# A decoder trunk on one core: a feed-forward in two phases with one wide matmul for both activation parts

## The chip, the cores and the metric

One core of one Trainium2 chip runs the whole program in one launch. The metric is device microseconds of one execution.

## What is computed

Four layers, each a feed-forward, a mixer and a second feed-forward, on 256 tokens of 1024 channels in float32. The mixers are in turn a gated recurrence with a short convolution (RG), forgetting attention (fox), a causal convolution module with 31 taps (conv), and RG again. Cut to what matters here:

```python
D_MODEL = 1024; BATCH = 1; SEQ = 256; DEPTH = 4; D_FF = 2816; CV_KERNEL = 31

def _rms_norm(x, g):
    y = x * lax.rsqrt(jnp.mean(x * x, axis=-1, keepdims=True) + EPS)
    return y * g

def _swiglu(x, w_in, w_out):
    gate, up = jnp.split(x @ w_in, 2, axis=-1)
    return (jax.nn.silu(gate) * up) @ w_out

# layer i
x = x + 0.5 * _swiglu(_rms_norm(x), w_in_1, w_out_1)
x = x + Mixer_{i mod 3}(_rms_norm(x))
x = x + 0.5 * _swiglu(_rms_norm(x), w_in_2, w_out_2)
```

## The kernel before, in words

x lies transposed: eight blocks of 128 channels (partitions) by 256 tokens. A weight block is 128x128 and stays in TensorE while tokens stream through it, so one matmul has 256 columns. For float32 accuracy each float32 operand is split into a high part, which the matmul takes whole, and a low part, the rest. A product of a weight block and activations then takes three matmuls: high weights on high activations, high weights on low activations, low weights on high activations.

**Weights.** Two feeds bring them in the order of use: `wi` for input weights, 1 MB chunks [128x2048], and `wo` for output weights, 512 KB chunks [128x1024]. `split_steps` (L92) makes the high part on ScalarE (ACT, L105) and the low part on VectorE (DVE, L108) as raw minus high. Some chunks are split in parts of 1024 or 512 columns. `ahead` (L122) splits up to a given depth and issues the next loads on SyncE's queue.

**A feed-forward stage** (`ffn`, L373) has 22 steps. Step p computes the gate and up block of hidden block p: `in_unit` (L298, matmuls in `in_steps`, L292), 8 input blocks x 2 x 3 = 48 matmuls into one bank of PSUM; then `out_unit` (L332, matmuls at L317) of hidden block p - 3, 8 x 3 = 24 matmuls which add to the four banks `o0` to `o3`. Between them `evac` multiplies by the norm (L379, 128x512), takes Silu on ScalarE (L381), multiplies by up (L383) and splits the result in `yh` (L385, ScalarE) and `yl` (L386, VectorE). `out_tail` (L336) finishes the last two hidden blocks, updates x (L352) and prepares the next stage: high part of x (L198), square (L211), low part (L224), sum of squares (`acc`, L218, folded at L220).

**The norm.** The input matmuls take x without its norm; the scale of each token is applied in `evac`. `norm_stat` (L260) sums the squares over the partitions with a matmul of ones against `acc` (128x256, every partition gets the same sums), computes z (L266) and an inverse root by three rounds of Newton's method (L246, then L255 to L257) on 128x256. Only VectorE's L379 waits for that.

**Mixers.** RG and conv use `in_unit` and `out_unit` as well. RG's four taps are on VectorE (L490). In conv (L974) the 8 x 31 taps are shared: 105 on VectorE (L1007, L1009), 72 as a ScalarE scale (L1021) with a GpSimd add (L1023), 71 on TensorE (L1030) as float32 matmuls against diagonal matrices, which GpSimd builds in `conv_setup` (L967) during the feed-forward before. `centre` (L1094) subtracts the bias of the layer norm and the statistics matmuls follow (L1104). In fox, `v_unit` runs 512-column matmuls (L685): there activations are the stationary operand and weights stream. Its two loops over heads carry the splits of the next stage's chunks as side work (`next_weights`).

The order of the work is written out by hand in all of this: each engine runs its instructions in the order of the program, and `plan` gives the engines of each split.

Of the kernel before, what the change touches and what calls it, by code (L numbers as in the profile page):

```python
# [60 lines left out]
N_IN = DEPTH * 2 * NF + 2 * 8 + 12 + 8  # L61
N_OUT = DEPTH * 2 * NF + DEPTH * KD


class Feed:


    def __init__(self, nc, src, n, width, pool, raw_bufs, part_bufs, tag):
        self.nc, self.src, self.n, self.width = nc, src, n, width
        self.pool, self.raw_bufs, self.part_bufs, self.tag = pool, raw_bufs, part_bufs, tag  # L70
        self.raw, self.parts, self.plan, self.pieces, self.spare = {}, {}, {}, {}, {}
        self.nd = self.ns = self.nu = 0
# [14 lines left out]
    def cuts(self, i):  # L87
        n = self.pieces.get(i, 1)
        w = self.width // n
        return [slice(j * w, (j + 1) * w) for j in range(n)]  # L90

    def split_steps(self):  # L92

        nc, i = self.nc, self.ns
        self.load(i + 1)
        raw = self.raw.pop(i)
        hi, lo = (self.pool.tile([P, self.width], F32R, tag=self.tag + x, bufs=self.part_bufs,
                                 name=f"{self.tag}{x}{i}") for x in "hl")
        self.parts[i] = (hi, lo)
        self.ns += 1  # L100
        cast, rest = self.plan.get(i, ("act", "dve"))
        rest = nc.gpsimd if rest == "pool" else nc.vector
        for c in self.cuts(i):
            if cast == "act":
                nc.scalar.activation(hi[:, c], raw[:, c], AF.Copy)  # L105
            else:
                nc.vector.tensor_copy(hi[:, c], raw[:, c])
            rest.tensor_tensor(lo[:, c], raw[:, c], hi[:, c].bitcast(F32), op=ALU.subtract)  # L108
            yield

    def split(self, upto):
        while self.ns < min(upto, self.n):
            for _ in self.split_steps():
                pass

    def take(self):
        self.split(self.nu + 1)
        r = self.parts.pop(self.nu)
        self.nu += 1
        return r  # L120

    def ahead(self, depth):  # L122
        self.split(self.nu + depth)
        self.load(self.ns + self.raw_bufs)


class Trunk:
# [3 lines left out]
    def build(self, pools):  # L131
# [3 lines left out]
        self.seq = 0  # L135
        self.sq = {}
        self.fin = Feed(nc, self.ap["win"], N_IN, 2 * D, self.wpool, 2, 3, "wi")
        self.fout = Feed(nc, self.ap["wout"], N_OUT, D, self.wpool, 3, 3, "wo")
        self.x = [c.tile([P, 2, T], F32, name=f"x{b}") for b in range(4)]
        self.vec = c.tile([P, NVEC], F32, name="vec")  # L140
        for i, t in zip((2, 3), self.slabs(2)):
            self.fin.spare[i] = t[:, :2 * D]
# [3 lines left out]
        self.fin.pieces[0] = 4  # L146
        self.fin.load(1, lambda j: load_x(j) if j else None)
        self.fin.pieces[1] = 2
        self.fin.load(4)
        nc.sync.dma_start(self.vec[:, KD:], self.ap["vec"][:, KD:])  # L150
        self.fout.load(2)
# [4 lines left out]
        self.fin.plan[0] = FIRST  # L156
        self.fout.plan[0] = self.fout.plan[1] = ("act", "dve")
        first = self.fin.split_steps()
        for b in range(4):
            self.prep_hi(b, 0, False)  # L160
            next(first)
            self.prep_sq(b, 0, True)
            self.prep_lo(b, 0)
        for _ in first:
            pass
        self.fin.split(2)
        for s in range(self.nsub):
            l, part = divmod(s, 3)
            last = s == self.nsub - 1
            for i in (2, 3) if s else (3,):  # L170
                self.fin.plan[self.fin.nu + i] = ("act", "dve")
            if part != 1:
                hook = None
                if s == 0:
                    hook = self.setup_lambda()
                elif s + 1 < self.nsub and part == 0 and MIXERS[l][0] == 2:
                    hook = self.conv_setup()
                self.ffn(s, last, hook, 1 if s == 0 else 6)
            else:
                kind, slot = MIXERS[l]  # L180
                (self.rg, self.fox, self.conv)[kind](s, slot, last)

# [6 lines left out]
    def prep_hi(self, b, s, sq=True):  # L189

        nc = self.nc
        if b == 0:
            self.xh, self.xl = ([self.work.tile([P, 2, T], F32R, tag=f"x{p}{i}", bufs=1,
                                                name=f"x{p}{s}_{i}") for i in range(4)]
                                for p in "hl")
            self.acc = self.work.tile([P, 2, T], F32, tag="acc", bufs=1, name=f"acc{s}")
        for j in range(2):
            nc.scalar.activation(self.xh[b][:, j], self.x[b][:, j], AF.Copy,  # L198
                                 scale=self.v(f"norm{s}", 2 * b + j))
        if sq:  # L200
            self.prep_sq(b, s)

    def prep_sq(self, b, s, pool=False):
        nc = self.nc
        sq = self.acc
        if b:
            sq = self.work.tile([P, 2, T], F32, tag="sq", bufs=2, name=f"sq{s}_{b}")
        if pool:
            nc.gpsimd.tensor_tensor(sq, self.x[b], self.x[b], op=ALU.mult)
        else:  # L210
            nc.scalar.activation(sq, self.x[b], AF.Square)  # L211
        self.sq[b] = sq

    def prep_acc(self, b):

        nc = self.nc
        if b:
            nc.vector.tensor_tensor(self.acc, self.acc, self.sq[b], op=ALU.add)  # L218
        if b == 3:
            nc.vector.tensor_tensor(self.acc[:, 0], self.acc[:, 0], self.acc[:, 1], op=ALU.add)  # L220

    def prep_lo(self, b, s):
        for j in range(2):
            self.nc.vector.scalar_tensor_tensor(self.xl[b][:, j], self.x[b][:, j],  # L224
                                                self.v(f"norm{s}", 2 * b + j),
                                                self.xh[b][:, j].bitcast(F32),
                                                op0=ALU.mult, op1=ALU.subtract)
        self.prep_acc(b)

    def pr(self, shape=None):  # L230
        self.seq += 1
        return self.psum.tile(shape or [P, 2, T], F32, tag="pr", bufs=3, name=f"pr{self.seq}")

    def st(self, shape):
        self.seq += 1
        return self.psum.tile(shape, F32, tag="st", bufs=1, name=f"st{self.seq}")
# [23 lines left out]
    def norm_stat(self):  # L260

        nc = self.nc
        ps = self.st([P, T])
        nc.tensor.matmul(ps, self.ones, self.acc[:, 0], start=True, stop=True)
        z = self.tmp([P, T], "h", 2)
        nc.vector.tensor_scalar(z, ps, 1.0 / D, EPS, op0=ALU.mult, op1=ALU.add)  # L266
        self.r_b = self.rsqrt(z, [P, T], "r")

    def norm_start(self):
        self.fin.ahead(2)  # L270
        self.norm_stat()
# [8 lines left out]
    def xk(self, k):  # L280
        return self.xh[k // 2][:, k % 2], self.xl[k // 2][:, k % 2]

    def in_steps(self, ps, ahead=2):
        nc = self.nc
        hi, lo = self.fin.take()
        hi = hi.rearrange("p (k j c) -> p k j c", k=KD, j=2)
        lo = lo.rearrange("p (k j c) -> p k j c", k=KD, j=2)
        for k in range(KD):
            xh, xl = self.xk(k)
            for j in range(2):  # L290
                for i, (w, m) in enumerate(((hi, xh), (hi, xl), (lo, xh))):
# [3 lines left out]
            yield  # L295
        self.fin.ahead(ahead)

    def in_unit(self, hook=None, at=2, ahead=2):  # L298
        ps = self.pr()
        for k, _ in enumerate(self.in_steps(ps, ahead)):  # L300
            if hook and k + 1 == at:
                hook()
        return ps

    def bank(self, b):
        self.seq += 1
        return self.psum.tile([P, 2, T], F32, tag=f"o{b}", bufs=1, name=f"o{b}_{self.seq}")
# [3 lines left out]

    def out_mm(self, m, w, y, first, last, which=(0, 1, 2)):
        hi, lo = w
        yh, yl = y
        for i, (wt, mv) in enumerate(((hi, yh), (hi, yl), (lo, yh))):
# [5 lines left out]
    def out_steps(self, y, first, ahead=True, late=False):  # L321
        w = self.fout.take()
# [932 lines left out]
```

## Time and profile before

| | |
|---|---|
| runs | 2031.32 us median of 3 (2031.09 to 2031.87) |
| profiled execution | 2032.03 us |
| its span | 2030.3 us |
| mean granted clock of TensorE | 0.984 |
| busy, share of span | TensorE 96%, VectorE 68%, ScalarE 47%, GpSimd 6% |
| DMA | 338 MB, mean 167 GB/s |

The span runs from the first to the last instruction; 1.7 us of the execution lie outside it. A busy time is the sum over the engine's instructions, with overlaps counted once. In the rows, PE is TensorE, DVE VectorE, ACT ScalarE, POOL GpSimd. A granted clock of 1.00 is 2.4 GHz, 0.50 is 1.2 GHz.

### The profile page before, as it was taken

The page shows a single profiled execution, that of the slowest core. Times are in us where ns is not written, and L with a number is a line of the kernel's source. Part 1 is how long each engine was busy: PE and PEld are TensorE (multiplying, and loading weights), DVE is VectorE, ACT ScalarE, POOL GpSimd, SP SyncE. Part 2 cuts the span into 40 slices and gives each one's busy share as a digit, 9 for nine tenths or more (in the row PEclk, how much of TensorE's full clock was granted, in tenths as well). Part 3 has the DMA queues.
Part 4 walks back from the last instruction along what each step waited for, and adds up shares of the span by engine and source line. Part 5 has one row for each costly group of instructions (what it writes and reads, how often), then busy time and mean ns, then how long its engine had stood idle before and what let it go on. Part 6 is the DMA issues. An engine that isn't in the chain of part 4 may idle for free.

```text
span 2030.3 us, 36907 instructions
## 1 busy us (share of the span) xinstructions
PE 1955.5 (96%) x15618; PEld 1912.5 (94%) x15618; DVE 1389.9 (68%) x1909; ACT 952.2 (47%) x1258; POOL 121.2 (6%) x169
## 2 busy tenths in 40 slices
PE   7999979999999999999999998779999999979998
PEld 7999979999999986999999998579999999979998
DVE  6765996656655767765576568976656655897654
ACT  5444654444444445444354445464444444465442
POOL 1000000000000000700000006700000000000000
PEclk9999989999999999999999999879999999989999
DMA  6555335554555342355546533035554655335541
GB/s 247 211 190 189 135 125 205 192 186 146 207 208 179 117 165 73 117 216 189 189 152 218 187 136 125 1 126 206 193 183 144 213 202 184 141 113 201 213 179 63
DMA packets 63670, 338.35 MB, mean 167 GB/s; under 512 B 7184, under 2 KB 8336, under 8 KB 36368
## 3 DMA queue, kind: packets, MB, share of 16 engines
q1 hardware_dynamic: 63504, 335.98, 46.5%
q8 instruction: 123, 2.02, 0.4%
q14 instruction: 43, 0.35, 0.1%
HBM read 334.90 MB, written 1.05 MB: 165 GB/s over the span
## 4 chain that ended last, share of the span: by engine, by line
PE 82%; DVE 13%; ACT 3%; issue 2%; DMA 1%; POOL 0%; DVEq 0%; SPq 0%; ACTq 0%; POOLq 0%
PE pr L292 51%; PE o L317 28%; DVE s L1009 3%; DVE wil L108 2%; PE o L685 1%; ACT wih L105 1%; DVE wol L108 1%; DMA wir<-win 0%; DVE sg L256 0%; DVE sg L255 0%; DVE xl L224 0%; DVE ry L257 0%; PE st L759 0%; DVE s L512 0%; DVE s L517 0%
## 5 line engine op out<-in xcount | busy, mean ns | idle before, releaser
L292 PE MATMUL pr<-xh,wih 128*128 128x256 f32 x3328 | 948.2, 285 | 8.7 <-ACT wih L105 7.4
L292 PE MATMUL pr<-xh,wil 128*128 128x256 f32 x3328 | 943.9, 284 | 6.0 <-DVE wil L108 6.0
L292 PE MATMUL pr<-xl,wih 128*128 128x256 f32 x3328 | 943.7, 284 | 1.6 <-DVE xl L224 1.6
L292 PEld LDWEIGHTS pr<-xh,wih 128*128 128x128 f32 x3328 | 640.5, 192 | 13.0 <-ACT wih L105 7.4
L292 PEld LDWEIGHTS pr<-xh,wil 128*128 128x128 f32 x3328 | 640.5, 192 | 7.0 <-DVE wil L108 7.0
L108 DVE TENSOR_TENSOR wil<-wir,wih 128x2048 fp32r<-128x2048 f32 (+2 forms) x220 | 482.9, 2197 | 239.0 <-ACT wih L105 238.1
L292 PEld LDWEIGHTS pr<-xl,wih 128*128 128x128 f32 x3328 | 640.4, 192 | 2.6 <-DVE xl L224 2.1
L317 PE MATMUL o<-yh,woh 128*128 128x256 f32 x1664 | 476.1, 286 | 23.4 <-ACT yh L581 18.1
L317 PE MATMUL o<-yh,wol 128*128 128x256 f32 x1664 | 474.0, 285 | 0.0
L317 PE MATMUL o<-yl,woh 128*128 128x256 f32 x1664 | 469.8, 285 | 2.8 <-DVE yl L613 2.7
L105 ACT ACTIVATE wih<-wir 128x2048 fp32r<-128x2048 f32 (+2 forms) x220 | 400.9, 1823 | 50.0 <-PE pr L292 25.7
L381 ACT ACTIVATE sg<-gu 128x256 f32<-128x256 f32 x176 | 73.5, 418 | 696.5 <-DVE gu L379 696.5
L317 PEld LDWEIGHTS o<-yh,woh 128*128 128x128 f32 x1664 | 322.8, 194 | 28.6 <-ACT yh L581 18.5
L317 PEld LDWEIGHTS o<-yl,woh 128*128 128x128 f32 x1664 | 320.1, 194 | 3.6 <-DVE yl L613 3.6
L317 PEld LDWEIGHTS o<-yh,wol 128*128 128x128 f32 x1664 | 322.8, 194 | 0.0
L108 DVE TENSOR_TENSOR wol<-wor,woh 128x1024 fp32r<-128x1024 f32 x208 | 253.0, 1221 | 24.8 <-ACT woh L105 24.6
L105 ACT ACTIVATE woh<-wor 128x1024 fp32r<-128x1024 f32 x208 | 216.1, 1044 | 14.9 <-PE o L317 14.6
L379 DVE TENSOR_TENSOR gu<-pr,ry 128x512 f32<-128x512 f32 x176 | 121.2, 689 | 109.7 <-PE pr L292 109.0
L383 DVE TENSOR_TENSOR h<-sg,gu 128x256 f32<-128x256 f32 x176 | 75.0, 426 | 95.0 <-ACT sg L381 95.0
L386 DVE TENSOR_TENSOR yl<-h,yh 128x256 fp32r<-128x256 f32 x176 | 74.9, 426 | 94.4 <-ACT yh L385 94.4
L385 ACT ACTIVATE yh<-h 128x256 fp32r<-128x256 f32 x176 | 73.5, 418 | 95.8 <-DVE h L383 93.1
L1023 POOL TENSOR_TENSOR s<-s,h 128x256 f32<-128x256 f32 x46 | 47.2, 1026 | 390.1 <-ACT h L1021 386.9
(256 smaller groups left out, 1038.8 us busy)
## 6 DMA issues: line engine op xcount, KB each, us to landing
wir<-win SPq DMA_DIRECT2D x208, 1024.0 KB, 4.9
wor<-wout SPq DMA_DIRECT2D x208, 512.0 KB, 5.2
s<-win SPq DMA_DIRECT2D x2, 1024.0 KB, 10.8
s<-wg SPq DMA_DIRECT2D x2, 1024.0 KB, 6.0
x<-xT SPq DMA_DIRECT2D x4, 256.0 KB, 5.3
wir<-win SPq DMA_DIRECT2D x4, 256.0 KB, 4.9
wir<-win SPq DMA_DIRECT2D x2, 512.0 KB, 8.2
out_dram<-x SPq DMA_DIRECT2D x8, 128.0 KB, 2.2
```

The costliest lines, as they stand in the source:

```text
L105: nc.scalar.activation(hi[:, c], raw[:, c], AF.Copy)
L108: rest.tensor_tensor(lo[:, c], raw[:, c], hi[:, c].bitcast(F32), op=ALU.subtract)
L292: nc.tensor.matmul(ps[:, j], w[:, k, j], m, start=(k == 0 and j == 0 and i == 0), stop=(k == KD - 1 and i == 2), skip_group_check=True)
L317: self.nc.tensor.matmul(self.o[m // 2][:, m % 2], wt[:, m * P:(m + 1) * P], mv, start=(first and m % 2 == 0 and i == 0), stop=(last and i ...
L379: nc.vector.tensor_tensor(gu, ps.pop(p), self.rb(2), op=ALU.mult)
L381: nc.scalar.activation(sg, gu[:, 0], AF.Silu)
L383: nc.vector.tensor_tensor(h, sg, gu[:, 1], op=ALU.mult)
L385: nc.scalar.activation(yh, h, AF.Copy)
L386: nc.vector.tensor_tensor(yl, h, yh.bitcast(F32), op=ALU.subtract)
L685: nc.tensor.matmul(dst, a[:, tt * P:(tt + 1) * P], w[:, i, hf * 512:(hf + 1) * 512], start=(k == 0 and n == 0), stop=(k == KD - 1 and n == 2))
L1009: nc.vector.scalar_tensor_tensor(dst, hp[:, n, k:k + T], w(n, k), dst, op0=ALU.mult, op1=ALU.add)
L1023: nc.gpsimd.tensor_tensor(cv[:, n], cv[:, n], dst, op=ALU.add)
```

## The change

One feed takes the place of two: chunks of 1 MB in the order of use, three raw buffers, five buffers of parts, every chunk split in pieces of 1024 columns, high on ScalarE and low on VectorE. `plan` is gone; `feed.fill()` splits whatever the free buffers allow, and the load of chunk i + 3 is issued behind the last low of chunk i.

The high and the low part of an activation block lie side by side (`xp`, `y`: [128, 2, 256]). In the feed-forward stages `wide_mm` runs the high weights against both in one 512-column matmul and the low weights against the high part in one of 256 columns, into the first half of the same bank. Mixers keep three matmuls of 256 columns.

The feed-forward has two phases. Phase 1 runs the 22 input units without output matmuls and keeps all y in SBUF; phase 2 runs the output weights, half of the output channels at a time, 22 hidden blocks each. `evac` adds the two halves of a bank: a ScalarE copy of the low half, a VectorE add.

The norm is computed on token partitions: two 128x2 matmuls give the sums with tokens on partitions, z and the inverse root are on 128x2, and two transposes on TensorE and a ScalarE copy spread the result over the partitions (`norm_wide`).

In conv, tiles 0 to 3 are VectorE's (124 taps) and tiles 4 to 7 TensorE's (124); ScalarE makes the diagonals during the mixer, in a ring of 68 places.

```diff
+PIECE = 1024
+CHUNK = 2 * D
+RAW = 3
+PARTS = 5
+PE_TILES = (4, 5, 6, 7)
...
+    def norm_stat(self, ps):
+        for tt in range(TT):
+            nc.tensor.matmul(ps[:, 2 * tt:2 * tt + 2], self.acc[:, 0, tt * P:(tt + 1) * P],
+                             self.ones[:, :2], start=True, stop=True)
+        z = self.tmp([P, TT], "nz")
+        nc.vector.tensor_scalar(z, ps[:, :2 * TT:2], 1.0 / D, EPS, op0=ALU.mult, op1=ALU.add)
+        self.r_tok = self.rsqrt(z, [P, TT], "n")
+
+    def norm_wide(self, ps):
+        self.bcast_cols(ps, [self.r_tok[:, tt:tt + 1] for tt in range(TT)])
+        self.r_b = self.tmp([P, T], "ry")
+        self.nc.scalar.copy(self.r_b, ps[:, :T])
+
+    def norm_hooks(self, ps=None):
+        if ps is None:
+            pair = self.pair()
+            ps = pair[:, 0], pair[:, 1]
+        return {6: lambda: self.norm_stat(ps[0])}, {2: lambda: self.norm_wide(ps[1])}
...
+    def wide_mm(self, bank, w, y, first, last):
+        mm = self.nc.tensor.matmul
+        hi, lo = w
+        mm(bank, hi, y.rearrange("p a t -> p (a t)"), start=first, stop=False,
+           skip_group_check=True)
+        mm(bank[:, :T], lo, y[:, 0], start=False, stop=last, skip_group_check=True)
...
         def evac(p):
+            ps = pss.pop(p)
+            parts = feed.begin() if feed.room() else []
+            bc = self.tmp([P, 2, T], "bc", 2)
+            nc.scalar.activation(bc, ps[:, :, T:], AF.Copy)
+            if p:
+                y_high(p - 1)
+            if parts:
+                parts[0][0]()
+            flush()
             gu = self.tmp([P, 2, T], "gu", 2)
-            nc.vector.tensor_tensor(gu, ps.pop(p), self.rb(2), op=ALU.mult)
+            nc.vector.tensor_tensor(gu, ps[:, :, :T], bc, op=ALU.add)
+            nc.vector.tensor_tensor(gu, gu, self.r_b[:, None, :].to_broadcast([P, 2, T]),
+                                    op=ALU.mult)
             sg = self.tmp([P, T], "sg", 2)
             nc.scalar.activation(sg, gu[:, 0], AF.Silu)
+            if parts:
+                parts[1][0]()
+            if p:
+                y_low(p - 1)
+            if parts:
+                parts[0][1]()
+                late.append(parts[1][1])
...
+        order = [(hf, f) for hf in range(2) for f in range(NF)]
...
+        for c in range(0, len(order), 4):
+            w = feed.take()
+            part = order[c:c + 4]
...
-DVE_TAPS = [(0, 0, CK), (2, 0, CK), (5, 0, 23), (3, 10, 22), (5, 23, CK)]
-POOL_TAPS = [(1, 0, CK), (3, 0, 10), (4, 0, CK)]
-PE_TAPS = [(3, 22, CK), (6, 0, CK), (7, 0, CK)]
...
+        while nst[0] < KD:
+            new = run(ge, 6) + run(gd, 5)
+            stats()
```

Three places where the order of an engine's instructions changes. The names: `wh`, `wl` (before `wih`, `wil`) are high and low weights, `wr` raw ones, `xp` the activation parts, `acc` the sums of squares, `ny` the inverse root, `pp` and `pr` banks of PSUM.

TensorE, unit 1 of the feed-forward stage after the first RG mixer. Before:

```order
L292 MATMUL pr_3344<-xh_0_3214,wih_3088 128x256
L292 MATMUL pr_3344<-xl_0_3218,wih_3088 128x256
L292 MATMUL pr_3344<-xh_0_3214,wil_3089 128x256
L264 MATMUL st_3357<-acc_3222,ones 128x256
L292 MATMUL pr_3344<-xh_0_3214,wih_3088 128x256
L292 MATMUL pr_3344<-xl_0_3218,wih_3088 128x256
L292 MATMUL pr_3344<-xh_0_3214,wil_3089 128x256
```

After:

```order
L291 MATMUL pp_78<-xp_1_2698,wh_2567 128x512
L293 MATMUL pp_78<-xp_1_2698,wl_2568 128x256
L291 MATMUL pp_78<-xp_1_2698,wh_2567 128x512
L293 MATMUL pp_78<-xp_1_2698,wl_2568 128x256
L277 MATMUL pp_80<-ident,ny_2805 128x128 x2
L291 MATMUL pp_78<-xp_1_2698,wh_2567 128x512
L293 MATMUL pp_78<-xp_1_2698,wl_2568 128x256
L291 MATMUL pp_78<-xp_1_2698,wh_2567 128x512
```

Three matmuls a block have become two, and before there was only the statistics matmul (L264), whose sums no row of TensorE's uses. Now the transposes (L277), which read the result of the whole norm, stand between the blocks.

VectorE, start of the same stage, from the last sum of squares. Before:

```order
L218 TENSOR_TENSOR acc_3222<-acc_3222,sq_3_3280 128x512
L220 TENSOR_TENSOR acc_3222<-acc_3222 128x256
L108 TENSOR_TENSOR wil_3339<-wir_3197,wih_3338 128x2048
L108 TENSOR_TENSOR wil_3352<-wir_3199,wih_3351 128x2048
L266 TENSOR_SCALAR h_3359<-st_3357 128x256
L246 TENSOR_SCALAR ry_3361<-h_3359 128x256
L255 TENSOR_TENSOR sg_3362<-h_3359,ry_3361 128x256
L256 SCALAR_TENSOR_TENSOR sg_3362<-sg_3362,ry_3361 128x256
L257 SCALAR_TENSOR_TENSOR ry_3361<-sg_3362,ry_3361 128x256
```

After:

```order
L219 TENSOR_TENSOR acc_2680<-acc_2680,sq_3_2740 128x512
L221 TENSOR_TENSOR acc_2680<-acc_2680 128x256
L102 TENSOR_TENSOR wl_2758<-wr_2506,wh_2757 128x1024 x2
L102 TENSOR_TENSOR wl_2766<-wr_2573,wh_2765 128x1024 x2
L259 TENSOR_SCALAR nz_2803<-pp_80 128x2
L238 TENSOR_SCALAR ny_2805<-nz_2803 128x2
L247 TENSOR_TENSOR nt_2806<-nz_2803,ny_2805 128x2
L248 SCALAR_TENSOR_TENSOR nt_2806<-nt_2806,ny_2805 128x2
L249 SCALAR_TENSOR_TENSOR ny_2805<-nt_2806,ny_2805 128x2
```

Two lows of 2048 columns have become four of 1024 (two rows that stand for two each), and the norm behind them runs on two columns instead of 256; six more rows of Newton rounds follow in both.

VectorE, steady part of a feed-forward stage. Before:

```order
L108 TENSOR_TENSOR wil_4136<-wir_3949,wih_4135 128x2048
L108 TENSOR_TENSOR wol_4166<-wor_3884,woh_4165 128x1024
L379 TENSOR_TENSOR gu_4171<-pr_4086,ry_3361 128x512
L383 TENSOR_TENSOR h_4175<-sg_4173,gu_4171 128x256
L386 TENSOR_TENSOR yl_4178<-h_4175,yh_4177 128x256
```

After (phase 1, one unit):

```order
L416 TENSOR_TENSOR gu_3237<-pp_77,bc_3230 128x512
L417 TENSOR_TENSOR gu_3237<-gu_3237,ry_2835 128x512
L402 TENSOR_TENSOR y_114_2752<-h_3194,y_114_2752 128x256
L102 TENSOR_TENSOR wl_3229<-wr_3133,wh_3228 128x1024
L429 TENSOR_TENSOR h_3245<-sg_3240,gu_3237 128x256
L102 TENSOR_TENSOR wl_3229<-wr_3133,wh_3228 128x1024
```

The multiply by the norm (L379) has become an add (L416) and a multiply (L417), the low of y (L402, before L386) is that of the unit before, and a low of the weights stands between each pair of operations that ScalarE's work separates.

## Rows read from the trace of the kernel before

**Rows 1.** The page, chain of work that ended last, share of the span by engine.

```profile
PE 82%; DVE 13%; ACT 3%; issue 2%; DMA 1%; POOL 0%; DVEq 0%; SPq 0%; ACTq 0%; POOLq 0%
```

**Rows 2.** Windows (start, RG, feed-forward, fox, conv): length, busy us by engine, clock, DMA.

```profile
0.00:32.18 32.18, 21.07 (x147) 20.15 (x147) 24.31 (x34) 16.18 (x21) 5.55 (x12) 1.00 0.80 292
205.20:296.88 91.68, 79.29 (x612) 77.48 (x612) 83.47 (x136) 54.20 (x76) 4.68 (x13) 0.94 0.37 125
487.38:677.89 190.51, 190.51 (x1588) 190.46 (x1587) 121.22 (x139) 84.90 (x101) 0.00 (x0) 1.00 0.51 183
677.89:828.46 150.57, 146.89 (x959) 119.83 (x958) 109.32 (x289) 76.33 (x160) 17.87 (x38) 1.00 0.33 113
1210.26:1362.12 151.86, 121.49 (x757) 110.90 (x756) 133.20 (x208) 83.33 (x144) 71.06 (x70) 0.87 0.24 84
```

**Rows 3.** Timeline of PE where the fox mixer starts: start, length, engine, line, operation.

```profile
677.49 0.28 PE L317 MATMUL o<-yl,woh 128*128 128x256 f32 x1
677.61 0.28 PE L317 MATMUL o<-yh,wol 128*128 128x256 f32 x1
677.73 0.40 PE L685 MATMUL o<-wih,xh 128*128 128x512 f32 x1
...
684.33 0.39 PE L685 MATMUL o<-wil,xh 128*128 128x512 f32 x1
```

**Rows 4.** Timeline of DVE, a steady unit of a feed-forward stage.

```profile
1100.23 2.29 DVE L108 TENSOR_TENSOR wil<-wir,wih 128x2048 fp32r<-128x2048 f32 x1 [1.38 <-ACT wih L105]
1102.44 1.22 DVE L108 TENSOR_TENSOR wol<-wor,woh 128x1024 fp32r<-128x1024 f32 x1
1103.74 0.69 DVE L379 TENSOR_TENSOR gu<-pr,ry 128x512 f32<-128x512 f32 x1
1104.98 0.42 DVE L383 TENSOR_TENSOR h<-sg,gu 128x256 f32<-128x256 f32 x1 [0.54 <-ACT sg L381]
```

**Rows 5.** Timeline of DVE, start of a feed-forward stage after the RG mixer.

```profile
301.47 2.29 DVE L108 TENSOR_TENSOR wil<-wir,wih 128x2048 fp32r<-128x2048 f32 x1
304.50 2.29 DVE L108 TENSOR_TENSOR wil<-wir,wih 128x2048 fp32r<-128x2048 f32 x1 [0.74 <-ACT wih L105]
306.71 0.42 DVE L266 TENSOR_SCALAR h<-st 128x256 f32<-128x256 f32 x1
...
311.63 0.69 DVE L379 TENSOR_TENSOR gu<-pr,ry 128x512 f32<-128x512 f32 x1
```

**Rows 6.** Timeline of DVE in the fox mixer, operations on 128x32.

```profile
703.33 0.19 DVE L438 TENSOR_TENSOR lsf<-lsf,lsq 128x32 f32<-128x32 f32 x1
703.56 0.18 DVE L439 TENSOR_SCALAR lsf<-lsf 128x32 f32<-128x32 f32 x1
```

**Rows 7.** Timeline of PE in the conv mixer, after a wait.

```profile
1256.56 0.53 PE L292 MATMUL pr<-xh,wil 128*128 128x256 f32 x1 [2.31 <-DVE wil L108]
1256.89 0.42 PE L292 MATMUL pr<-xh,wih 128*128 128x256 f32 x1
...
1260.08 0.28 PE L292 MATMUL pr<-xh,wih 128*128 128x256 f32 x1
```

**Rows 8.** Timeline of DVE, start of the kernel.

```profile
19.88 4.48 DVE L108 TENSOR_TENSOR wil<-s,wih 128x2048 fp32r<-128x2048 f32 x2
24.28 0.42 DVE L266 TENSOR_SCALAR h<-st 128x256 f32<-128x256 f32 x1
```

**Rows 9.** Groups of instructions, shapes apart: lows of a quarter chunk.

```profile
L108 DVE TENSOR_TENSOR wil<-wir,wih 128x512 fp32r<-128x512 f32 x12 | 8.2, 686 | 12.1 <-ACT wih L105 11.9
```

**Rows 10.** Timelines of DVE: taps of the RG mixer, then taps of the conv mixer.

```profile
221.87 2.46 DVE L490 SCALAR_TENSOR_TENSOR s<-s,vec,s 128x256 f32<-128x256 f32 x6
...
1297.51 10.08 DVE L1009 SCALAR_TENSOR_TENSOR s<-s,vec,s 128x256 f32<-128x256 f32 x12
```

**Rows 11.** Timeline of PE, taps of the conv mixer.

```profile
1282.74 2.97 PE L1030 MATMUL pr<-s,s 128*128 128x256 f32 x13
```

**Rows 12.** Waits of PE: who was waited for, us in total, times, longest.

```profile
PE st L1104 <- DVE s L1094: 10.8, 4, 4.1
```

More of the change, by code (lines that the diff above doesn't have):

```diff
@@ L406, in ffn @@
-        for k in range(NF - lag, NF - 2):
-            self.out_unit(ys.pop(k), False)
-        self.out_tail([ys.pop(NF - 2), ys.pop(NF - 1)], s, last, 0.5)
+            if p:
+                evac(p)
+            if hook and p > 2:
+                next(hook, None)
+        if hook:
+            for _ in hook:
+                pass
+        y_high(NF - 1)
+        y_low(NF - 1)
+        flush()
+        obs = [[self.pair(), self.pair()] for _ in range(2)]
+        order = [(hf, f) for hf in range(2) for f in range(NF)]
@@ new lines, in ffn @@
+        for c in range(0, len(order), 4):
+            w = feed.take()
+            part = order[c:c + 4]
+            if c + 4 < len(order):
+                for i, e in enumerate(part):
+                    for m in range(4):
+                        out_mm(e, i, m, w)
+                if (0, NF - 1) in part:
+                    for m in (0, 2):
+                        update(0, m, 2)
+                    if not last:
+                        self.prep_lo(0, s + 1)
+                        self.prep_lo(1, s + 1)
+                feed.fill()
+                continue
+            todo = []
+            for m in range(4):
+                for i, e in enumerate(part):
+                    out_mm(e, i, m, w)
+                update(1, m, 1)
+                if not last:
+                    for t in todo:
+                        self.prep_lo(*t)
+                    todo = [(2 + m // 2, s + 1, (m % 2,))]
+            for t in todo:
+                self.prep_lo(*t)
@@ L549, in rg @@
         lift(3)
-        self.fin.ahead(3)
         taps(3)
+        feed.fill(1)
         for n in range(4):
@@ L556, in rg @@
         ps[4] = self.in_unit()
-        self.fin.ahead(3)
+        feed.fill(1)
+        for n in range(4, 8):
+            gates(n)
+        evac_g(0)
         recip(0)
@@ new lines, in pe_taps @@
+        def pe_taps():
+            for i, (n, k) in enumerate(pe_order):
+                if k == 0:
+                    pcs[n] = self.pr()[:, 0]
+                nc.tensor.matmul(pcs[n], room[i % len(room)], hp[:, n, k:k + T],
+                                 start=(k == 0), stop=(k == CK - 1))
+                diagonals(i + 1 + len(room))
+                yield n if k == CK - 1 else None
+        gd, ge = dve_taps(), pe_taps()
+        def run(gen, n):
+            return [r for r in (next(gen, None) for _ in range(n)) if r is not None]
@@ L1077, in conv @@
             value(n - 1)
-            if n < 6:
-                self.fin.ahead(2)
-            note([run(gp, CV_IN[2]), None, run(gd, CV_IN[1] if n > 2 else 0)])
-            note([None, None, early])
-        note([run(gp, 4), run(ge, 12), run(gd, 6)])
-        self.warm(AF.Ln)
+            diagonals(8 * n)
+            feed.fill(1)
+            if n > 2:
+                run(gd, 2)
+        done, pend, todo = 0, [], []
+        cb = self.tmp([P, T], "cb")
         cps = self.bank(1)[:, 0]
-        nc.tensor.matmul(cps, self.ones, cv[:, 1], start=True, stop=True)
@@ L1106, in stats @@
                 nst[0] += 1
[L1108 to L1122 removed]
+            pend.clear()
+        known = False
+        while nst[0] < KD:
+            new = run(ge, 6) + run(gd, 5)
+            stats()
+            todo += new
+            if not known and 0 in todo:
+                known = True
+                nc.tensor.matmul(cps, self.ones, cv[:, 0], start=True, stop=True)
+                nc.scalar.mul(cb, cps, 1.0 / P)
+                continue
+            if known:
+                for n in todo[:2]:
+                    centre(n)
+                todo = todo[2:]
+        self.warm(AF.Ln)
         m2, z = (self.tmp([P, 2, T], "gu", 2)[:, 0] for _ in range(2))
```

719 lines of the change are left out of this document (313 added, 406 removed).

## The prediction

> **What bounds the kernel now.** I read the chain of work that ended last first. TensorE holds 82% of it, VectorE 13% [rows 1], so the time is the time TensorE needs plus the places where it stands. The windows by stage show where that is [rows 2]: a feed-forward stage between two others is 190.51 us long and TensorE is busy for 190.50 of them, while VectorE is busy for 121 and ScalarE for 85. The eight such stages are three quarters of the span and nothing but TensorE sets their length. The mixers differ: in the RG mixer TensorE is busy 79 of 92 us and VectorE 83, in the conv 121 of 152 and VectorE 133; the fox mixer has TensorE busy for 147 of 151.
>
> Next, what one matmul costs. In 190.50 us there are 22 units of 48 input and 24 output matmuls with 256 columns, 1584 in all, so 120 ns each; the matmul rows show the same step (677.49, 677.61, 677.73) [rows 3]. Where the fox mixer runs 512 columns, 29 steps from 677.73 to 684.33 take 6.60 us, 227.6 ns each [rows 3]. Twice the columns cost 107.6 ns more, so about 12 to 13 ns of each matmul does not grow with its columns. That is the number on which the change rests.
>
> **The feed-forward matmuls: -56 us.** A weight block took three matmuls, 3 x 120 = 360 ns. Now the high weights meet [high | low] in one 512-column matmul and the low weights meet the high half: 227 + 120 = 347 ns, 13.3 ns less. A stage has 22 x 24 = 528 blocks, the kernel 8 x 528 = 4224: 4224 x 13.3 = 56.3 us. I take it whole, because the row of the 512 shape is of the same type of operand and the same clock. At 12.4 ns it would be 52. A rule speaks against it. The Trainium skill (TensorE: Matmul & The Clock Gate, section Back-to-back issue gap) gives a warm gap of the columns over 2.4 GHz plus 2.5 ns. By that only 2.5 ns a block would be saved, 10.6 us in all; the rows disagree, at 120 and 227 ns against its 109 and 216.
>
> **Does VectorE keep up?** Phase 1 is 22 units with no output matmuls between them, so TensorE needs 16 x 347 ns = 5.55 us a unit, where VectorE had 8.64 us before. Per unit VectorE now has one add and one multiply of 128x512 (0.69 us each), two operations of 128x256 (0.42 each) and two lows of 128x1024 (1.22 each) [rows 4]: 4.66 us by durations, some 4.2 by starts, as neighbours overlap by about 0.08 us (1100.23 to 1102.44 for an operation of 2.29). The order puts a low or an old y between the operations that wait for ScalarE, so the 0.54 us that VectorE stood before h and before y_low [rows 4] should be filled. With 1.3 us to spare it costs nothing. The cover is thin; if it goes, the first rival below follows. Phase 2 has 61 us for eleven chunks' lows, 25 us of VectorE. DMA moves the same bytes at about the same rate.
>
> **The norm: now TensorE waits, +19 us.** Before, only VectorE's first 128x512 multiply (311.63) waited for the eleven operations of the norm; TensorE ran on into other banks [rows 5]. Now two transposes stand in TensorE's own queue in unit 1, after 16 + 6 blocks, 22 x 347 = 7.63 us into the stage, and every later matmul is queued behind them. What they wait for: the fold of the squares, which ends 4.6 us after a mixer's last matmul (296.88 to 301.47) [rows 2, 5]; then by the order four lows of 1.14 us, 4.55; then eleven tiny operations. Such tiny ones start 0.23 us apart [rows 6] (the norm's are smaller still: 0.19 to 0.23), about 2.1 us. Together 11.2 us, so TensorE stands 3.6 us. A stand of 2.31 us was followed by half speed, 213 ns a matmul, from 1256.56 to 1260.08 [rows 7], which cost 3.5 x (1 - 120/213) = 1.5 us. One such stand need not halve the clock; I take 0.9. Four feed-forward stages follow a mixer: 4 x 4.5 = 18, between 14 (no half clock) and 21. After a feed-forward, whose tail is split finer, and in the mixers, two lows stand there instead of four: 7.7 us against 7.6, +1 for all. With every wait covered it would be nothing, the lower end.
>
> **The start: +4.** In the first stage the same chain began at 24.28, behind the lows of four chunks [rows 8], with three units under way. Now five chunks' lows stand ahead, the fifth loaded only when a buffer is free, so the chain ends near 28 and TensorE, in unit 1, waits for it from about 22. The third unit then ends near 35, not 32.2; some of that is in the matmul term. From 0 to +8.
>
> **RG mixers: -8.** VectorE is busy 83 of 92 us [rows 2]. The norm chain, 306.71 to 311.63 or 4.9 us on 256 columns [rows 5], shrinks to 2.2 us, and lows in halves wait less for ScalarE (0.74 before one) [rows 5]. Some 4 us in each of two; ends 0 and -6 each.
>
> **Fox: +3.** Eight lows of 128x512 in the head loops, 0.69 us [rows 9], become 128x1024 ones of 1.22, 8 x 0.53 = 4.3 us more on VectorE inside a chain of heads; half or more shows. Ends -1 and +7.
>
> **Conv: -13.** GpSimd's taps go. VectorE's taps start 0.83 us apart (twelve in 10.08) while GpSimd adds; the RG mixer's, without it, 0.40 (six in 2.46) [rows 10]. VectorE gets 124 taps, about 30 within the input units; the rest, 94 x 0.40 = 37 us, lies beside TensorE's own 124 taps, 248 passes 0.216 us apart (13 in 2.97) [rows 11], 53.5 us. The stage then is the input 128 x 0.36 = 46.1, the taps 53.5, the statistics and tail about 14 (TensorE no longer stands 10.8 us for VectorE's centred tiles [rows 12]) and the output 64 x 0.36 = 23 plus 1.5 until the clock is up: 138 against 151.9 [rows 2]. ScalarE makes the diagonals, 124 small copies, beside it. I take -13, ends 0 (the tail waits as before) and -20.
>
> **The sum.** -56.3 + 18 + 1 + 4 - 8 + 3 - 13 = -51.3 on the profiled execution's 2032.0 (span 2030.3 and 1.7 around it) gives 1980.7. The median shown is 0.7 lower, so 1980.
>
> **Rivals.**
> VectorE bounds phase 1 (slower). If the interleaving does not hide ScalarE, each unit costs VectorE 4.2 us plus two stands of 0.54 and one of 0.74: 6.0 us. That is 0.45 over TensorE's 5.55, times 176 units, 80 us: 2060. It decides from 5.84 us a unit, where the 51 us are eaten (51 / 176 = 0.29). For it: VectorE stands at every such place now [rows 4]. Against: the new order has work in each place. Chance 0.09.
> The fixed part is not saved. If a 512-column matmul between 256-column ones takes 240 ns, as two of 256 do, the 56.3 us go and the time is 2036. Nothing in the rows speaks for it: 29 steps of that shape are 227.6 ns each [rows 3]. Chance 0.04, with all that lies between. By the Trainium skill's 2.5 ns (the page and section above) it would be 2026; no row here agrees.
> Every stage start waits. If the feed has four lows, not two, ahead of the norm at the seven other starts, TensorE stands 3.6 + 1.5 there too: 7 x 5.1 = 36 less the 1 counted: 2015. For it: the feed splits whatever buffers are free. Chance 0.10.
> The waits are hidden and the mixers gain most: no 19 at the starts, conv -20: 1954. Chance 0.05.
>
> **How the numbers follow.** My forecast keeps 0.72. The range 1956 to 2015 takes in its ends and most of the third rival and leaves out the others, 0.18. A measurement here can tell about 0.2%, 4 us. Faster: 0.72 + 0.10 + 0.05 and 0.01 of the second rival, 0.88; same: 0.02 of it; slower: its last 0.01 and the first rival's 0.09, 0.10.
>
> **What would show it.** A steady phase 1 unit of 5.55 us with 512 columns at 227 ns and TensorE without gaps; feed-forward stages near 183 us plus the wait at their start; four gaps of 3 to 4 us before the transposes, released by VectorE; RG near 87, conv near 139, fox near 153. Wrong: VectorE busy without a break in phase 1 with TensorE standing before each unit, or 512-column steps that differ from the fox mixer's.

## The result, and the profile after

The changed kernel takes 2122.26 us (median of 4 runs, 2116.99 to 2130.61) against 2031.2 before: a ratio of 1.0452, 95% interval 1.0417 to 1.0488. I forecast 1980, with 0.88 for faster. The profiled execution is the longest of the four: span 2128.9 us, some 98.6 more than before.

First the chain of the changed kernel by engine, from its page, to set beside [rows 1]. It tells little here: TensorE still holds most of it, and a share of the chain does not tell work at full clock from work at half clock.

```profile
PE 83%; DVE 9%; ACT 5%; issue 2%; DMA 1%; SPq 0%; ACTq 0%; DVEq 0%
```

The windows by stage do tell, in the columns of [rows 2]: RG, a feed-forward behind a feed-forward, fox, conv.

```profile
214.29:317.52 103.23, 85.16 (x616) 80.97 (x615) 78.09 (x139) 52.87 (x81) 0.00 (x0) 0.90 0.32 113
513.96:706.71 192.75, 188.90 (x1064) 163.75 (x1063) 134.44 (x191) 99.14 (x147) 0.00 (x0) 0.99 0.52 181
706.71:901.62 194.91, 168.78 (x960) 136.39 (x959) 104.15 (x290) 75.76 (x163) 4.01 (x15) 0.87 0.23 81
1286.14:1443.24 157.10, 137.53 (x867) 127.18 (x865) 106.34 (x229) 85.80 (x201) 0.00 (x0) 0.93 0.20 74
```

Against [rows 2] the fox mixer alone lost 194.91 - 150.57 = 44.3 us, the first RG mixer 11.6, conv 5.2, and the feed-forward, which was to gain seven, lost 2.2. Fox has the same matmuls as before (960 against 959), and VectorE and ScalarE are no busier there. Its loss has two halves, which the same rows give: TensorE is idle for 26.1 us instead of 3.7 (length less busy time), 22.5 more, and the same matmuls are busy 21.9 us longer, as the granted clock fell from 1.00 to 0.87. So the loss is waiting, and the half clock that goes with it. TensorE's waits over the whole kernel (who was waited for, total, times, longest):

```profile
PE pp L291 <- DVE x L474: 29.0, 16, 2.9
PE pp L277 <- DVE ny L249: 17.6, 5, 7.4
PE pp L314 <- DVE s L622: 17.2, 2, 9.2
PE pp L594 <- ACT s L597: 11.3, 8, 2.9
PE pp L939 <- ACT s L930: 8.1, 7, 2.8
PE pp L291 <- ACT wh L99: 7.8, 2, 7.2
```

L622 and L594/L597 are in the RG mixers, L939 and L930 in fox; L277 are the norm's transposes. The first wait is in no part of my sum. L474 is the update of x at the end of phase 2. Here it is in the timeline of TensorE (first fence) and of VectorE (second), at the end of the first feed-forward stage behind RG:

```profile
503.82 0.40 PE L291 MATMUL pp<-y,wh 128*128 128x512 f32 x1
504.05 0.28 PE L293 MATMUL pp<-y,wl 128*128 128x256 f32 x1
507.21 0.50 PE L291 MATMUL pp<-y,wh 128*128 128x512 f32 x1 [2.88 <-DVE x L474]
507.55 0.28 PE L293 MATMUL pp<-y,wl 128*128 128x256 f32 x1
```

```profile
504.00 2.36 DVE L102 TENSOR_TENSOR wl<-wr,wh 128x1024 fp32r<-128x1024 f32 x2 [3.25 <-ACT wh L99]
506.28 0.88 DVE L474 SCALAR_TENSOR_TENSOR x<-pp,x 128x256 f32<-128x256 f32 x2
```

The last matmul of output block 0 starts at 504.05. Block 1 goes to another bank and reads nothing that the update writes, and yet it starts only at 507.21, when VectorE has finished reading block 0, behind two lows. Block 0 and block 1 are two banks of one PSUM tile. The weights of block 1 lie in the chunk that block 0 had just used, and the y are the same, so it did not wait for these. The half clock that follows lasts 3.4 us (508.70:512.10 has a granted clock of 0.50). The 16 waits are two a stage: seven of 2.9 us and nine of about 1.0. Six of the seven long ones were followed, or overlapped, by half clock.

The step of the matmuls in phase 1, to set beside [rows 3]: four blocks from 539.61 to 541.01 take 1.40 us; over the 282 blocks between 530 and 630 us it is 353.3 ns a block (512 columns 236.7, 256 columns 116.7), not 346.7.

```profile
539.61 0.40 PE L291 MATMUL pp<-xp,wh 128*128 128x512 f32 x1
539.84 0.28 PE L293 MATMUL pp<-xp,wl 128*128 128x256 f32 x1
...
541.01 0.40 PE L291 MATMUL pp<-xp,wh 128*128 128x512 f32 x1
```

And VectorE in one unit of phase 1, to set beside [rows 4]: 5.65 us from add to add, which is 16 blocks of 353.3 ns, with one idle place of 1.29 us, before the add. VectorE keeps up.

```profile
560.64 0.69 DVE L416 TENSOR_TENSOR gu<-pp,bc 128x512 f32<-128x512 f32 x1 [1.30 <-ACT bc L409]
561.36 0.69 DVE L417 TENSOR_TENSOR gu<-gu,ry 128x512 f32<-128x512 f32 x1
561.97 0.42 DVE L402 TENSOR_TENSOR y<-h,y 128x256 fp32r<-128x256 f32 x1
562.31 1.22 DVE L102 TENSOR_TENSOR wl<-wr,wh 128x1024 fp32r<-128x1024 f32 x1
563.44 0.42 DVE L429 TENSOR_TENSOR h<-sg,gu 128x256 f32<-128x256 f32 x1
563.78 1.22 DVE L102 TENSOR_TENSOR wl<-wr,wh 128x1024 fp32r<-128x1024 f32 x1
566.29 0.69 DVE L416 TENSOR_TENSOR gu<-pp,bc 128x512 f32<-128x512 f32 x1 [1.29 <-ACT bc L409]
```

### The profile page after: what moved, and what is told of

It reads as the page before. It is cut to its first block, busy times and chain, and to the rows that moved or that the text cites. A ratio compares the mean times of both kernels' runs of the same rounds, so it can differ in the third digit from the quotient of the medians.

```text
span 2128.9 us, 28810 instructions
## 1 busy us (share of the span) xinstructions
PE 1986.3 (93%) x11546; PEld 1734.1 (81%) x11546; DVE 1461.3 (69%) x2379; ACT 1076.4 (51%) x1720; POOL 5.4 (0%) x25
## 3 DMA queue, kind: packets, MB, share of 16 engines
q1 hardware_dynamic: 48240, 335.97, 44.3%
## 4 chain that ended last, share of the span: by engine, by line
PE 83%; DVE 9%; ACT 5%; issue 2%; DMA 1%; SPq 0%; ACTq 0%; DVEq 0%
PE pp L291 44%; PE pp L293 23%; PE pp L314 6%; DVE wl L102 4%; PE pp L342 3%; PE pp L1085 2%; ACT wh L99 1%; PE pp L780 1%; PE pp L594 1%; DVE s L1077 1%; DVE x L474 1%; ACT s L1051 1%; PE pp L939 0%; ACT s L604 0%; PE pp L277 0%
## 5 line engine op out<-in xcount | busy, mean ns | idle before, releaser
L291 PE MATMUL pp<-xp,wh 128*128 128x512 f32 x2816 | 997.8, 399 | 7.8 <-ACT wh L99 7.8
L102 DVE TENSOR_TENSOR wl<-wr,wh 128x1024 fp32r<-128x1024 f32 (+1 forms) x634 | 758.8, 1217 | 295.5 <-ACT wh L99 295.5
L293 PE MATMUL pp<-xp,wl 128*128 128x256 f32 x2816 | 792.7, 281 | 1.4 <-DVE wl L102 1.4
L99 ACT ACTIVATE wh<-wr 128x1024 fp32r<-128x1024 f32 (+1 forms) x634 | 649.0, 1046 | 239.6 <-issue 187.1
L291 PEld LDWEIGHTS pp<-xp,wh 128*128 128x128 f32 x2816 | 531.4, 189 | 135.6 <-ACT wh L99 8.3
L293 PEld LDWEIGHTS pp<-xp,wl 128*128 128x128 f32 x2816 | 534.7, 190 | 2.8 <-DVE wl L102 2.8
L291 PE MATMUL pp<-y,wh 128*128 128x512 f32 x1408 | 506.8, 402 | 29.0 <-DVE x L474 29.0
L293 PE MATMUL pp<-y,wl 128*128 128x256 f32 x1408 | 400.5, 284 | 0.0
L291 PEld LDWEIGHTS pp<-y,wh 128*128 128x128 f32 x1408 | 268.9, 191 | 98.7 <-DVE x L474 34.9
L293 PEld LDWEIGHTS pp<-y,wl 128*128 128x128 f32 x1408 | 269.4, 191 | 0.0
L416 DVE TENSOR_TENSOR gu<-pp,bc 128x512 f32<-128x512 f32 x176 | 121.6, 691 | 183.7 <-ACT bc L409 183.2
L314 PE MATMUL pp<-xp,wh 128*128 128x256 f32 x1024 | 202.8, 300 | 30.7 <-DVE s L622 17.2
L314 PEld LDWEIGHTS pp<-xp,wh 128*128 128x128 f32 x1024 | 171.4, 205 | 36.3 <-DVE s L622 17.6
L314 PE MATMUL pp<-xp,wl 128*128 128x256 f32 x512 | 151.4, 296 | 0.0
L417 DVE TENSOR_TENSOR gu<-gu,ry 128x512 f32<-128x512 f32 x176 | 121.8, 692 | 6.0
L314 PEld LDWEIGHTS pp<-xp,wl 128*128 128x128 f32 x512 | 105.2, 205 | 0.0
L474 DVE SCALAR_TENSOR_TENSOR x<-pp,x 128x256 f32<-128x256 f32 (+1 forms) x96 | 48.4, 511 | 54.3 <-PE pp L293 52.7
```

Of the source, the lines that this page charges most:

```text
L102: nc.vector.tensor_tensor(lo[:, c], raw[:, c], hi[:, c].bitcast(F32), op=ALU.subtract)
L291: mm(bank, hi, y.rearrange("p a t -> p (a t)"), start=first, stop=False, skip_group_check=True)
L293: mm(bank[:, :T], lo, y[:, 0], start=False, stop=last, skip_group_check=True)
L314: nc.tensor.matmul(ps[:, j], w[:, k, j], m, start=(k == 0 and j == 0 and i == 0), stop=(k == KD - 1 and i == 2), skip_group_check=True)
L416: nc.vector.tensor_tensor(gu, ps[:, :, :T], bc, op=ALU.add)
L417: nc.vector.tensor_tensor(gu, gu, self.r_b[:, None, :].to_broadcast([P, 2, T]), op=ALU.mult)
```

## Experiments

**Theory A:** the new PSUM layout is the cause. Four tiles of two banks (`pp`) hold everything; whoever writes one bank of a tile waits until the other has been read. Before, every bank was a tile. **Theory B:** the waits are real, VectorE and ScalarE are late because lows and casts stand ahead of what TensorE needs.

### One bank per tile

```diff
-        self.pp = [self.psum.tile([P, 2, 2 * T], F32, tag=f"pp{i}", bufs=1, name=f"pp{i}")
-                   for i in range(4)]
+        self.pp = [[self.psum.tile([P, 2 * T], F32, tag=f"pp{i}{j}", bufs=1, name=f"pp{i}{j}")
+                    for j in range(2)] for i in range(4)]
...
-            nc.scalar.activation(bc, ps[:, :, T:], AF.Copy)
+            for j in range(2):
+                nc.scalar.activation(bc[:, j], ps[j][:, T:], AF.Copy)
...
-            nc.vector.tensor_tensor(gu, ps[:, :, :T], bc, op=ALU.add)
+            for j in range(2):
+                nc.vector.tensor_tensor(gu[:, j], ps[j][:, :T], bc[:, j], op=ALU.add)
```

> The changed kernel with eight PSUM tiles of one bank in place of four tiles of two banks; the copy, the add and the x update that took both banks in one instruction are now one per bank. Theory A (waits between the two banks of one tile): a matmul into one bank waits until ScalarE or VectorE has read the other bank of its tile, though no data ties them. Then the 16 waits at L474 (29.0 us) and the half clock behind them (8 x 1.7 us) go, some 43 us, and the RG and fox mixers lose 30 to 45 us more: 2122 - 80 = about 2040, the fox stage near 160 us instead of 195. Theory B (the waits are real: VectorE and ScalarE are late because lows and casts stand ahead of the work that TensorE needs): the waits stay, 2105 to 2125, the fox stage stays above 185.

Measured: 2024.51 us (9 runs), ratio to before 0.9953 (0.9937 to 0.997). 98 us less than the changed kernel, from an edit that only adds instructions. The waits that are left, then the windows (RG, feed-forward, fox, conv):

```profile
PE pp L277 <- DVE ny L249: 22.2, 11, 7.1
PE pp L342 <- ACT yp L682: 17.6, 2, 8.8
PE pp L1149 <- DVE s L1080: 9.8, 1, 9.8
PE pp L291 <- ACT wh L99: 7.2, 1, 7.2
```

```profile
204.49:294.04 89.55, 78.33 (x616) 76.69 (x615) 78.47 (x143) 52.67 (x83) 0.00 (x0) 0.94 0.41 151
483.31:670.97 187.66, 187.11 (x1065) 162.50 (x1063) 135.68 (x218) 101.05 (x170) 0.00 (x0) 1.00 0.51 185
670.97:828.27 157.30, 148.75 (x960) 120.61 (x959) 103.71 (x294) 74.86 (x166) 3.27 (x15) 0.98 0.30 107
1207.46:1360.06 152.60, 135.58 (x867) 125.87 (x865) 106.72 (x232) 86.14 (x204) 0.00 (x0) 0.94 0.23 82
```

The waits on L597 are gone, and of those on the x update and on L930 0.6 and 0.4 us are left. Fox fell by 37.6 us, RG by 13.7, conv by 4.5, this feed-forward by 5.1. Theory A holds, and for more than I had put on it. The wait is one of the program, which guards a tile as a whole, not one of the banks: the same banks, as tiles of their own, do not have it. The waits on L622 are an exception. Two of 8.8 us on L682, further on in the RG mixer, have come in their place, and the kernel before had a pair of 9.1 there too; what RG gained comes from its other waits and from less half clock.

### The same wait, moved by order alone

The edit above also changes instruction sizes. So, with the two-bank tiles, only the order of the last four output blocks:

```diff
             todo = []
-            for m in range(4):
+            for m in (0, 2, 1, 3):
```

> The changed kernel with its two-bank tiles, and one edit: in the last chunk of phase 2 the four output blocks come in the order 0, 2, 1, 3, so that each next block lies in the other tile. Theory (a matmul waits for the reading of its tile's other bank): block 2 does not wait at all, block 1 waits about 1.6 us for the update of block 0 instead of 2.9, block 3 not at all. Per stage 2.7 us less, and in most the half clock behind it (1.7 us) too: 8 x 2.7 to 4.4 = 22 to 35 us, 2087 to 2100. Rival (the next matmul waits for VectorE whatever the bank): 2118 to 2126.

Measured: 2091.78 us (4 runs), 30.5 less than the changed kernel. The wait on the x update, in TensorE's list, is now

```profile
PE pp L291 <- DVE x L474: 10.3, 7, 1.5
```

instead of 29.0 us in 16 waits: seven waits of 1.5 us, one a stage but the last, where the expectation had 1.6. Block 2, whose tile nobody reads, starts at once, and block 1 waits for what is left of the update. That is theory A's pattern; theory B has no place for it.

### What the wide matmul saves

```diff
-        mm(bank, hi, y.rearrange("p a t -> p (a t)"), start=first, stop=False,
-           skip_group_check=True)
+        mm(bank[:, :T], hi, y[:, 0], start=first, stop=False, skip_group_check=True)
+        mm(bank[:, T:], hi, y[:, 1], start=False, stop=False, skip_group_check=True)
```

> The changed kernel with each wide 512-column matmul of the feed-forward split back into two of 256 columns, all else kept. By my forecast a block is 360 instead of 347 ns, 13.3 ns x 4224 = +56 us: about 2178. By the trace of the changed kernel a block takes 353 ns, so 7 ns x 4224 = +30: about 2152. If phase 1 is set by VectorE or DMA and not by TensorE, it stays at 2122.

Measured: 2150.06 us (4 runs), 27.8 more: 6.6 ns a block, as 360 - 353.3 says. Its steps in phase 1 are 120 ns, all 832 of them between 530 and 630 us:

```profile
539.84 0.28 PE L291 MATMUL pp<-xp,wh 128*128 128x256 f32 x1
539.96 0.28 PE L292 MATMUL pp<-xp,wh 128*128 128x256 f32 x1
540.08 0.28 PE L293 MATMUL pp<-xp,wl 128*128 128x256 f32 x1
```

So TensorE sets phase 1, and the wide matmul is worth 28 us of the 56 forecast.

Is the missing half due to the alternation of widths? On the one-bank kernel, in pairs of banks:

```diff
-        mm(bank, hi, y.rearrange("p a t -> p (a t)"), start=first, stop=False,
-           skip_group_check=True)
-        mm(bank[:, :T], lo, y[:, 0], start=False, stop=last, skip_group_check=True)
+        for bank, w in zip(banks, ws):
+            mm(bank, w[0], y.rearrange("p a t -> p (a t)"), start=first, stop=False,
+               skip_group_check=True)
+        for bank, w in zip(banks, ws):
+            mm(bank[:, :T], w[1], y[:, 0], start=False, stop=last, skip_group_check=True)
```

> The kernel with one-bank tiles, and in the feed-forward matmuls the order 512, 512, 256, 256 columns over two banks instead of 512, 256, 512, 256. A block takes 353.3 ns in phase 1 where I forecast 346.7. If the 6.7 ns come from the alternation of widths, two of four changes go and the block falls by 3 to 7 ns: 4224 x 3 to 7 = 13 to 28 us, 1996 to 2012. If they belong to each 512-column matmul beside other engines' work, the block stays at 353 and the time at 2024.

Measured: 2015.69 us (4 runs), 8.8 less than with one bank per tile, a little above the lower theory's band. In its phase 1 two blocks take 696.7 ns on the mean (143 pairs), 348.4 each:

```profile
540.12 0.62 PE L290 MATMUL pp<-xp,wh 128*128 128x512 f32 x2
540.58 0.40 PE L293 MATMUL pp<-xp,wl 128*128 128x256 f32 x2
540.81 0.63 PE L290 MATMUL pp<-xp,wh 128*128 128x512 f32 x2
541.28 0.39 PE L293 MATMUL pp<-xp,wl 128*128 128x256 f32 x2
```

Most of what I missed per block was the alternation: 4.9 of 6.7 ns. Over 4224 blocks that is 20.7 us, and 8.8 came. The waits at the transposes explain little of the rest (22.5 us in all instead of 22.2); the mean granted clock is lower, 0.983 in the profile against 0.986, by an estimate 0.003 x 2014 = 6 us. Why it is lower was not tested. A wide matmul still steps at 233, not 227, beside another; why stays open.

### The norm one unit later

```diff
-                else:
-                    hooks = wide
+            elif p == 2 and s:
+                hooks = wide
...
-            if p == 1:
+            g = 2 if s else 1
+            if p == g:
                 feed.fill(1)
-                evac(0)
-            if p:
+                for i in range(g):
+                    evac(i)
+            if p >= g:
                 evac(p)
```

> The changed kernel with the two transposes of the norm one unit later (unit 2 in place of 1) in all feed-forward stages but the first, and the evacuations of units 0 and 1 behind it. If the wait at the transposes is only a matter of place, the four waits of 2.5 us behind mixers and their half clock (3.4 us at half speed, 1.7 lost) go: 4 x 4.2 = 17 us, about 2105. If VectorE is then late with the evacuations instead, the wait moves to unit 3 or 4 and the time stays at 2122.

Measured: 2112.33 us (4 runs), 9.9 less. Of the five waits at the transposes one is left, the one at the start, which this edit does not move:

```profile
PE pp L277 <- DVE ny L249: 8.3, 1, 8.3
```

The waits went as the theory says, and none came back at the evacuations. The gain is nearer to the waits alone (4 x 2.5) than to waits and half clock (17). In the profile of the changed kernel only two of the four waits had half clock with them, so about 4 x 2.5 + 2 x 1.7 = 13.4 was to be had; with its runs between 2117 and 2131 us these can't be told apart well.

### Fox: shorter lows in the chain of the heads

```diff
+        for i in range(feed.ns, feed.ns + 2):
+            feed.pieces[i] = 4
         heads(0, ("o0", "o1", "o2", "o3"), late_qk(), (2, 1), True, feed.steps(1))
```

> The changed kernel with the two chunks that are split inside the first loop over heads of the fox mixer in pieces of 512 columns instead of 1024, as before the change. If the longer lows in the chain of the heads are what the fox mixer lost, the stage falls from 195 us to 180 or less: about 2107. If the loss is in waits between banks, it falls by 5 us at most: 2117 to 2122.

Measured: 2124.03 us (4 runs), no difference. The lows of 1024 columns were not what fox lost. The same edit with one bank per tile:

> The kernel with one-bank tiles, and the two chunks split in the first loop over heads of the fox mixer in pieces of 512 columns, as before the change. The fox stage is 157.3 us there against 150.6 before. If the longer lows in the chain of heads are the difference, it falls to 152 or 153: about 2020. If not, within 1 us of 2024.5.

Measured: 2026.91 us (10 runs), against 2024.51: nothing gained. The fox stage is 162.1 us in its profile, where that of the one-bank kernel is 157.3, and 159.6 and 157.1 in the kernels with casts first and with three parts together (both below); so this stage varies by some us between profiles. Of the 6.7 us that remain against 150.6 in the one-bank kernel's profile, 4.9 are more idle time, and one wait of 5.1 us (L314 on L846, ScalarE's) has no counterpart in the kernel before; 1.9 are a lower clock (0.98). Why ScalarE is late there was not tested.

### Conv: casts ahead of the diagonals

In the changed kernel VectorE comes to its taps late. ScalarE's timeline in one input unit of the conv, and VectorE's low behind it:

```profile
1318.78 2.43 ACT L1051 ACTIVATE s<-ident,vec 128x128 f32<-128x128 f32 x8
1321.12 1.99 ACT L99 ACTIVATE wh<-wr 128x1024 fp32r<-128x1024 f32 x2
```

```profile
1322.19 2.36 DVE L102 TENSOR_TENSOR wl<-wr,wh 128x1024 fp32r<-128x1024 f32 x2 [2.34 <-ACT wh L99]
```

On the one-bank kernel:

```diff
-            diagonals(8 * n)
             feed.fill(1)
+            diagonals(8 * n)
```

> The kernel with one-bank tiles, and in the conv mixer's input units the casts and lows of the next chunk ahead of the eight diagonals in ScalarE's queue, instead of behind them. Theory: the diagonals (8 x 0.31 us) make every low late, VectorE stands 2.3 us a unit in six units and comes to its taps 14 us late, for which TensorE stands 9.8 us at the layer norm's first statistics (L1149) and runs at half clock behind it. Then the conv stage falls from 152.6 to 138 to 143 us: 2024.5 - 12 = about 2012. Rival: VectorE's 124 taps are too many wherever ScalarE's work lies; the stage stays above 149: 2021 to 2025.

Measured: 2010.45 us (4 runs), 14.1 less; the stage, from its windows:

```profile
1211.83:1351.93 140.10, 132.89 (x866) 124.33 (x865) 107.14 (x232) 87.32 (x204) 0.00 (x0) 0.98 0.25 90
```

The wait of 9.8 us at the first statistics is gone. My conv term's size (138 us) was right for a kernel whose ScalarE queue is in this order.

### The parts together

One bank per tile, the norm one unit later in every feed-forward stage, casts ahead of diagonals:

> The kernel with one-bank tiles, the norm's transposes one unit later in all feed-forward stages (the first too), and the conv mixer's casts ahead of the diagonals. If the parts add: the wait of 7.1 us at the start shrinks to 2 or less (-5 to -8 with its half clock), the four waits of 3.4 us and their half clock go (-17), four of 0.8 us (-3), conv -12: 2024.5 - 38 = about 1986. If waits that go come back at the evacuations of units 0 to 2: 2000 to 2010.

Measured: 1993.64 us (4 runs), ratio 0.9804 (0.9779 to 0.9828). At the start 3.3 us are left at the transposes and a wait of 2.9 us came back, at the evacuations (L291 on L418); in all it is 8 us less gain than I forecast. With the grouped order as well:

> One-bank tiles, transposes one unit later, casts ahead of diagonals, and matmuls in the order 512, 512, 256, 256. The grouped order took 8.8 us off the kernel with one-bank tiles and brought a phase-1 block from 353.3 to 348.4 ns. If that adds to the 1993.6 us of the other three: 1980 to 1986. If phase 1 at the shorter block is met by VectorE (about 5 us of work in 5.57 us a unit), TensorE stands before units and the time stays at 1990 to 1994.

Measured: 1978.83 us (5 runs), ratio 0.9738 (0.9718 to 0.9758): 1 us below the faster of the two. VectorE does not stand in the way: one wait of 1.4 us at an evacuation is left. What TensorE still waits for most:

```profile
PE pp L341 <- ACT yp L681: 17.6, 2, 8.8
PE pp L290 <- ACT wh L99: 7.8, 2, 7.2
PE pp L341 <- ACT yp L1187: 6.3, 1, 6.3
```

These are RG, the end of conv and the start, and the kernel before had each of them in like size:

```profile
PE o L317 <- ACT yh L581: 18.1, 2, 9.1
PE pr L292 <- ACT wih L105: 7.4, 1, 7.4
PE o L317 <- ACT yh L1155: 5.3, 1, 5.3
```

## Why the prediction was wrong, point by point

- **"The new order has work in each place" (first rival): right.** VectorE keeps to 5.65 us a unit with 1.3 to spare, so the rival that I gave 0.09 did not happen. The kernel did come out slower, but for a cause that I had not named, so the 0.10 that I left for slower is no credit to the forecast.
- **"Fox: +3" and "RG mixers: -8": wrong, and the step that failed.** They measured +44.3, +11.6 and +9.8. I priced what the mixers execute (lows, the norm chain) and put the change of their PSUM banks at nothing, without a reason. The step I left out is the layout: the mixers' banks for input products, output products and statistics (`prb`, `ob`, `stb`) are now halves of four shared tiles, and a bank is written only after its neighbour has been read. Giving each bank its own tile brought fox to 157.3 and RG to 89.6 and 90.0, near and below [rows 2], and the kernel from 2122.3 to 2024.5.
- **The end of phase 2: a missing term.** The same wait costs 29.0 us in 16 places, two lows on VectorE in front of it make it long, and a stretch at half clock (3.4 us at 0.50 behind the one shown) goes with six of the seven long ones. By the order alone 30.5 us came back.
- **"The feed-forward matmuls: -56 us": the sign right, half the size.** Measured 28 us. The 227 ns of [rows 3] hold where 512-column matmuls follow each other; between matmuls of 256 columns they are 236.7 (and 256 columns 116.7). By the gap that the Trainium skill (TensorE: Matmul & The Clock Gate, section Back-to-back issue gap) gives for an isolated matmul, columns over 2.4 GHz and 2.5 ns, a block is an estimated 215.8 + 109.2 = 325 ns; the trace has 353.3, and the trace decides. That share of 2.5 ns a matmul does not hold here, as [rows 3] already showed.
- **"The norm: now TensorE waits": right, size a little high.** VectorE's four lows and eleven tiny operations stand in front as I laid out. In the changed kernel behind the first RG mixer, VectorE's lows start at 321.58, z at 326.12, and TensorE resumes at 328.30 after 2.52 us; I forecast 3.6. The chain ended 10.8 us into the stage, not 11.2, and TensorE, at 353 ns a block, came later. Half clock went with two of the four such waits; I had allowed 0.9 us each for it. In the first feed-forward it waited 7.4, where I had about 6. The third rival (all stage starts wait as much) did not happen: five waits in the changed kernel, 17.6 us. With one bank per tile the four behind mixers are 3.1 us each, nearer to my 3.6, and six others are 0.4 to 0.6.

```profile
321.58 4.62 DVE L102 TENSOR_TENSOR wl<-wr,wh 128x1024 fp32r<-128x1024 f32 x4
326.12 0.15 DVE L259 TENSOR_SCALAR nz<-pp 128x2 f32<-128x2 f32 x1
```

```profile
328.30 0.69 PE L277 MATMUL pp<-ident,ny 128*128 128x128 f32 x2 [2.52 <-DVE ny L249]
```

- **"Conv: -13": wrong as built, right for the parts.** I costed the diagonals at nothing, as "beside it" on ScalarE. They were ahead of the casts in ScalarE's queue, so each low came 2.3 us late and VectorE's taps with it. The cover was there, the order was not: 140.1 us once the casts come first.

Of the 142 us between my 1980 and the 2122 measured, 98 went with the one-bank tiles. The 44 that were left are, by these points, 28 of the matmul term, 14 of conv, 4 of fox and 4 to 5 of RG; that adds to some 50, so the starts and the norm came out about 6 us cheaper than I had them. This last is a difference, not a measurement.

With the PSUM tiles apart, the norm later, the casts first and the matmuls grouped, the kernel takes 1978.8, close to the 1980 of my sum; but this is another kernel than the one I priced, and the sum has terms that cancel (half the matmul gain, less waiting), so that nearness is luck and no proof of it.

## What to carry to other kernels

Where a change rearranges PSUM or SBUF into bigger tiles, list for each tile who writes and who reads its parts, and look for a writer of one part that follows a reader of another: here that was a new wait though no data tied the two, and it cost 98 us. When work is "beside" the path on some engine, look at what stands behind it in that engine's own queue. Price a mixed stream of matmul widths from a row of that mixture, not from a row of each width among its own kind.

## What the runs showed that I had not expected

Alternating 512 and 256 columns makes a block 353.3 ns, three matmuls of 256 columns 360, and two 512 followed by two 256 columns 348.4 a block; by rows among their own kind it would be 347. The 512-column steps in the alternating stream repeat as 241, 236 and 233 ns, some 94 times each in 100 us. And half clock went with waits of TensorE shorter than 3 us, but not with each: with six of seven of 2.9 us and two of four of 2.5 to 2.7 us; the one of 2.88 us that ended at 507.21 was followed by 3.4 us at 0.50.
